# Second layer of a decoder trunk: the queries of three of eight heads formed by seven block products

## The chip, the cores and the metric

The kernel runs on one core of a Trainium2 chip. The metric is device time in microseconds (us) of one execution; a kernel is run several times and the median is given. Four engines matter here. TensorE (PE) multiplies matrices, and its weight loads have a row of their own in the profile (PEld). VectorE (DVE) and ScalarE (ACT) do elementwise work and alone empty the accumulators that TensorE writes. GpSimd (POOL) has a small part. SyncE (SP) issues most of the transfers (DMA).

## The reference

Sixteen learned meta tokens and 512 real ones, 1024 wide, pass through two layers with a residual, each behind an RMS norm: gated linear attention (GLA), then differential attention. A last RMS norm follows. The change lies in the second layer:

```python
proj = xn @ w_in                                  # 528 x 1024 by 1024 x 8192
q, k, v, z = jnp.split(proj, 4, axis=-1)          # 2048 columns each, 256 per head
s = einsum('bhpqd,bhpkd->bhpqk', qb, kh) * d**-0.5 + bias     # d = 128, p = 2 maps per head
p = softmax(s); a = p[:, :, 0] - lam * p[:, :, 1]
o = head_rms(a @ vh) * gnorm * (1 - lambda_init)
y = silu(z) * o;  h = h + y @ w_out
```

There are eight heads. A head has two query maps of 128 columns, and q of a head is the product of the normed tokens (1024 inputs) with 256 columns of `w_in`, scaled by -128 ** -0.5. Meta tokens need no queries in the second layer, as their output rows are dropped, so q has 512 tokens.

## The kernel before, in words

**Precision.** All products are of fp32 values split into a high part and a low rest, both in the type fp32r (`split`, L270). Three passes make a product: high by high, high by low, low by high.

**Two ways to form a projection.** The plain way is `project` (L414): the weights of 128 output columns lie in SBUF as a pair of tiles (high, low) of 8 slices, and for each slice three matmuls run over 512 token columns into one accumulator. A head's q has two such halves, 48 matmuls. The parts are prepared by `halves_of` (two pairs per load).

The other way is the class `Unit` (L436) over `product` (L428). The inputs are cut in two (512 of 1024), the output columns in two (128 of 256) and the tokens in two (an upper and a lower half). The 2 x 2 by 2 x 2 block product is then done by seven products of sums of blocks instead of eight products of blocks. Each product is 4 slices x 3 passes = 12 matmuls; its columns are half the tokens: 256 for real tokens only (the set `Xr`), 264 with the meta tokens (the set `X`). The sums of token blocks are made once for the layer. The sums of weight blocks are made for each unit by `want_unit` (L356): three single blocks (a11, a12, a22) are split, four additions on VectorE form sums, and two pairs of sums (s21, s43) are split. The products end in the accumulators bx, by and bv; `partial` copies three running results out of bx to tiles u on ScalarE (L452), and `add` combines accumulators and partials on VectorE into the output tile (L477, L479). When both token halves of one output block are there, `tail` is called. If the next piece of work in the queue is a unit too, its first product (a11) is issued ahead of the last two products of the running one.

**The order of the work.** TensorE's order is written out by the program. The projections stand in a queue as generators (the `Weaver`): each attention step of a head is emitted, and between two steps `W.fill` takes a number of microseconds of projection work, by the generators' own estimates, out of the queue. During head n the queue holds: the output projection of heads n-2 and n-1 (for n = 2, 4, 6), then z, v, k and q of head n+1; in head 6 the order is k, q, v, z. `W.stop` holds k and q back until the scores of head n are out, as k and q have one set of tiles. A head begins by finishing its own q (`W.finish(projs[hd])`), then takes 3.0 estimated us of the next work, and then emits its first scores, which need all of q and k. ScalarE, VectorE and the transfers are put in order by a planner from priorities: `at_once`, `urgent`, `soon` move an instruction 160, 100 or 40 places ahead of its place in the program.

**The weights.** `Weights` keeps the jobs in the order in which they are wanted. The two foremost are loaded into two buffers `raw`; their parts are made as soon as their buffers are free (two pairs, one sum, one each of a11, a12, a22), strictly in order. A transfer is issued from SP.

**The steps that are touched.** `q_diff_q` (L1650) forms q the plain way for all heads; each half is split straight out of its accumulator (ScalarE L279, VectorE L280). `q_diff_k` is a unit for heads 1 to 7 and shows what such a unit's ending looks like: `add` into temporary tiles `t` (three buffers, `tok_tile`), then `split` under `soon`. In this text heads are counted by index 0 to 7, so the fourth, sixth and eighth head are heads 3, 5 and 7, and their q are formed during heads 2, 4 and 6.

Of the kernel before, what the change touches and what calls it, by code (L numbers as in the profile page):

```python
# [12 lines left out]
F32R = mybir.dt.float32r  # L13
# [7 lines left out]
P = 128  # L21
# [3 lines left out]
NR = 512  # L25
# [184 lines left out]
def trunk(ctx, tc, x, meta, g_norm, gla_w_in, gla_w_gate_up, gla_b_gate, gla_gnorm, gla_w_out,  # L210
# [9 lines left out]
    d_w_in, d_lam, d_gn, d_w_out = diff_w_in[0], diff_lam[0], diff_gnorm[0], diff_w_out[0]  # L220
# [11 lines left out]
    def T(p, shape, dt, tag, **kw):  # L232
        uid[0] += 1
        return p.tile(shape, dt, tag=tag, name=f"{tag}_{uid[0]}", **kw)

    def pb_tile(tag):
        return T(pb_pool, [P, 512], F32, tag, bufs=2 if tag == "bx" else 1)
# [10 lines left out]
    def by_halves(t):  # L248
        return t.rearrange("p (n c) -> p n c", n=2)
# [4 lines left out]
    def urgent(fn, offset=100):  # L254

        def run(*a, **kw):
            with tc.high_priority(offset=offset):
                return fn(*a, **kw)
        return run
# [10 lines left out]
    def split(hi, lo, src, scale=None, keep=False):  # L270

        if keep:
            act.activation(hi, src, AF.Copy)
            kept.append(lambda: dve.tensor_tensor(lo, src, hi.bitcast(F32), op=ALU.subtract))
        elif scale is None:
            act.activation(hi, src, AF.Copy)  # L276
            dve.tensor_tensor(lo, src, hi.bitcast(F32), op=ALU.subtract)  # L277
        else:
            act.activation(hi, src, AF.Copy, scale=scale)  # L279
            dve.scalar_tensor_tensor(lo, src, scale, hi.bitcast(F32), op0=ALU.mult, op1=ALU.subtract)  # L280
# [21 lines left out]
    def block(raw, b):  # L302
        i, j = divmod(b, 2)
        return raw[:, 4 * j:4 * j + 4, i * P:(i + 1) * P]

    def in_rows(t):
        return t.rearrange("p (k c) -> p k c", c=P)

    W = Weaver()
# [22 lines left out]
    def halves_of(c):  # L332
        return [Part("pair", lambda raw, ca=ca: split_w(raw, ca)) for ca in (0, c)]
# [11 lines left out]
    def block_pair(src, keep=False):  # L345
        wh, wl = w_pair([P, 2, 512])
        if src.shape[1] == 2:
            split(wh, wl, src, keep=keep)
        elif src.shape[1] == 8:
            split(*[t.rearrange("p i (k c) -> p (i k) c", c=P) for t in (wh, wl)], src, keep=keep)  # L350
        else:
            split(*[t.rearrange("p i (k c) -> p i k c", c=P) for t in (wh, wl)],
                  src.rearrange("p k (i c) -> p i k c", c=P), keep=keep)
        return [[t[:, i, :] for t in (wh, wl)] for i in range(2)]

    def want_unit(w, c0, calm=False):  # L356
        def single(tag, b):
            def fn(raw):
                t = [T(wp, [P, 512], F32R, tag + part, bufs=1) for part in "hl"]
                with tc.issue_after(W.moved.ins) if calm and b == 0 else ExitStack():  # L360
                    split(*[in_rows(o) for o in t], block(raw, b))
                return t
            return Part(tag, fn)

        def add(o, a, b):
            dve.tensor_tensor(o, a, b, op=ALU.add)

        def sums(raw):
            t = T(wp, [P, 2, 512], F32, "sum", bufs=1)
            add(in_rows(t[:, 1, :]), block(raw, 2), block(raw, 3))  # L370
            add(in_rows(t[:, 0, :]), in_rows(t[:, 1, :]), block(raw, 0))
            add(block(raw, 2), block(raw, 2), block(raw, 0))
            return t

        def outer(raw):
            add(block(raw, 0), block(raw, 1), in_rows(su.t[:, 0, :]))
            ws.room["sum"] += 1
            return block_pair(raw[:, :4, :])

        a11, a12, a22 = single("a11", 0), single("a12", 1), single("a22", 3)  # L380
        su = Part("sum", sums)
        s21 = Part("pair", lambda raw: block_pair(su.t))
        s43 = Part("pair", outer)
        ws.want((w, c0), [a11, su, s21, a12, s43, a22])
        return a11, a12, a22, s21, s43
# [28 lines left out]
    def project(w, xs, n0, nn, banks, ks=range(KT)):  # L414

        (wh, wl), (xh, xl) = w.t, xs
        nk = wh.shape[1]
        todo = [(k, wh, b) for k in ks for b in (xh, xl)] + [(k, wl, xh) for k in ks]
        for n, (k, a, b) in enumerate(todo):
            for i, bank in enumerate(banks):  # L420
                pe.matmul(bank, a[:, k, :], b[k] if n0 is None else b[k][:, n0 + i * nn:n0 + (i + 1) * nn],  # L421
                          start=n == 0 and ks[0] == 0, stop=n == len(todo) - 1 and ks[-1] == nk - 1)
            if n % 3 == 2:
                yield 3 * len(banks) * max(nn / 2400.0, 0.107)
        if ks[-1] == nk - 1:
            ws.done(w)
# [211 lines left out]
    for b in range(5):  # L638
        t0, n = BLK[b]
        t = T(gp, [P, D], F32, ("qs", "ks")[b - 1]) if b in (1, 2) else {0: z2, 3: v2[0], 4: v2[1]}[b][:, 1, :]  # L640
# [134 lines left out]
    for k0 in range(0, KT, 2):  # L775
        if k0 + 2 < KT:
            scaled_pair(k0 + 2)
        i, ks = k0 // 4, slice(k0 % 4, k0 % 4 + 2)
# [204 lines left out]
    heads = [Head() for _ in range(G_HEADS)]  # L983
# [359 lines left out]
    for hd in range(G_HEADS):  # L1343
        s = heads[hd]
# [121 lines left out]
    def want_diff(c):  # L1466
        ws.want_in_order((d_w_in, 0, KT, c), halves_of(P))
# [29 lines left out]
    ep = ctx.enter_context(tc.tile_pool(name="ep", bufs=2))  # L1497
# [39 lines left out]
    Xr = {}  # L1537
# [8 lines left out]
    heads = [Head() for _ in range(D_HEADS)]  # L1546
# [16 lines left out]
    def tok_tile():  # L1563
        return T(ep, [P, 2 * (256 + NM)], F32, "t", bufs=3)
# [83 lines left out]
        return W.add(gen(), 10.3)  # L1648

    def q_diff_q(hd, s):  # L1650
        want_diff(256 * hd)

        def gen():
            for i in range(2):
                bank = pb_tile("bx" if hd else ("bv", "by")[i])
                yield from project(ws.take(), real2, None, NR, [by_halves(bank)])
                assert not hd or heads[hd - 1].scored
                if i == 0:
                    s.q = [T(ep, [P, 2, NR], F32R, f"q{j}", bufs=1) for j in range(2)]
                urgent(split)(*[t[:, i, :] for t in s.q], bank, scale=-float(P) ** -0.5)  # L1660
        return W.add(gen(), 10.3)

    def diff_steps(hd, s, ys):
# [156 lines left out]
    s = heads[0]  # L1820
# [5 lines left out]
    ws.room["sum"] += 1  # L1826
    s.T = bias_tile(0)
    q_diff_q(0, s)
    W.fill(2.5)
    for i in range(5):  # L1830
# [4 lines left out]
    for hd in range(D_HEADS):  # L1835
        last = hd == D_HEADS - 1
        s = heads[hd]
# [7 lines left out]
        if not last:  # L1845
            n = heads[hd + 1]
            late = hd == D_HEADS - 2
            if not late:
                gates.append(q_diff_z(hd + 1, n))
                values.append(q_diff_v(hd + 1, n))  # L1850
            W.stop = q_diff_k(hd + 1, n)
            projs.append(q_diff_q(hd + 1, n))
            if late:
                values.append(q_diff_v(hd + 1, n))
                gates.append(q_diff_z(hd + 1, n))
# [96 lines left out]
```

## Time and profile before

| | |
|---|---|
| median of 3 runs | 972.43 us (972.37 to 973.35) |
| profiled execution | span 970.2 us from first to last instruction; the page gives no other time of it |
| TensorE busy | 957.1 us (99%), 6993 matmuls |
| VectorE busy | 778.4 us (80%) |
| ScalarE busy | 628.0 us (65%) |
| matmuls of `project` with 512 columns, high weights, into bx (L421) | 224 |
| second layer, first scores of heads 0 to 7 | at 500.1, 552.3, 604.9, 678.7, 731.9, 805.3, 858.5, 913.1 us |

How to read it: busy time is the union of an engine's instructions. Matmuls overlap in the records (a row's length runs from its start to its modelled end), so the cost of one in a run is taken from start to start. A row `L431 PE MATMUL bx<-x,wh 128*128 128x256 f32 x8` reads: line 431, TensorE, into accumulator bx, from tiles x and wh, 128 by 128 weights, 256 columns, eight of them. In the list of waits a row names who waited, for whom, the total, the number and the longest, in us. In a table of stretches the numbers after the stretch are its length and each engine's busy time with its instructions, then the granted clock, the share of the transfer engines and GB/s.

### The profile page before, as it was taken

How to read it: one execution, taken by the hardware profiler on the slowest of the kernel's cores; microseconds unless marked ns; L12 is line 12 of the kernel's file. 1: busy time of each engine (PE TensorE's matmuls, PEld its weight loads, DVE VectorE, ACT ScalarE, POOL GpSimd, SP SyncE). 2: the span in 40 equal slices, each digit the busy share in tenths (PEclk: the TensorE clock that was granted, in tenths of full speed). 3: DMA queues.
4: the chain of work that ended last, by engine and by line, in shares of the span. 5: the costliest groups of instructions: out<-in, count | busy, mean ns of one | idle time of the engine just before them, and what ended most of it. 6: DMA issues, size and time to landing. Idle time of an engine off the chain costs nothing. (4 is left out here: it accounts for less than half of the span.)

```text
span 970.2 us, 18065 instructions
## 1 busy us (share of the span) xinstructions
PE 957.1 (99%) x6993; PEld 906.5 (93%) x6993; DVE 778.4 (80%) x1586; ACT 628.0 (65%) x1304; POOL 50.6 (5%) x68
## 2 busy tenths in 40 slices
PE   8999999999999999999999999999999999999997
PEld 8999999999999999898899998898998999989996
DVE  7989885886888887568997985977958879677785
ACT  7776755577647567656757774576764677655583
POOL 1000000000000100000001001001010000000001
PEclk9999999999999999999999999999999999999999
DMA  7322223635363245224355525135252352412212
GB/s 197 88 86 60 79 81 122 148 99 129 120 156 96 79 121 154 62 92 151 100 132 147 131 78 153 51 97 140 86 148 88 99 138 86 148 61 84 87 66 87
DMA packets 128521, 104.94 MB, mean 108 GB/s; under 512 B 51101, under 2 KB 112829, under 8 KB 128432
## 3 DMA queue, kind: packets, MB, share of 16 engines
q1 hardware_dynamic: 123104, 93.80, 35.1%
q10 hardware_dynamic: 5328, 9.95, 2.8%
q8 instruction: 56, 0.92, 0.4%
q14 instruction: 33, 0.27, 0.1%
HBM read 83.64 MB, written 11.80 MB: 98 GB/s over the span
## 5 line engine op out<-in xcount | busy, mean ns | idle before, releaser
L277 DVE TENSOR_TENSOR wl<-raw,wh 128x1024 fp32r<-128x1024 f32 x98 | 119.5, 1222 | 24.8 <-ACT wh L276 16.8
L276 ACT ACTIVATE wh<-raw 128x1024 fp32r<-128x1024 f32 x98 | 103.2, 1055 | 52.6 <-PE by L968 23.2
L431 PE MATMUL bv<-x,wh 128*128 128x264 f32 (+1 forms) x656 | 97.6, 286 | 0.0
L431 PE MATMUL bx<-x,wh 128*128 128x264 f32 (+1 forms) x640 | 94.9, 286 | 0.7 <-ACT u L452 0.6
L431 PEld LDWEIGHTS bv<-x,wh 128*128 128x128 f32 x656 | 86.5, 188 | 0.6 <-DVE z L479 0.3
L431 PEld LDWEIGHTS bx<-x,wh 128*128 128x128 f32 x640 | 84.5, 188 | 1.9 <-ACT u L452 1.2
L452 ACT ACTIVATE u<-bx 128x264 f32<-128x264 f32 (+1 forms) x120 | 45.4, 380 | 32.3 <-PE bx L431 31.1
L421 PE MATMUL bx<-x,wh 128*128 128x512 f32 (+1 forms) x256 | 62.4, 386 | 0.0
L277 DVE TENSOR_TENSOR wl<-sum,wh 128x1024 fp32r<-128x1024 f32 x41 | 50.1, 1221 | 14.3 <-ACT wh L276 13.9
L431 PE MATMUL bv<-x,wl 128*128 128x264 f32 (+1 forms) x328 | 55.2, 285 | 0.1
L1718 POOL TENSOR_TENSOR st<-st,mhalf 128x1 f32<-128x1 f32 x32 | 31.0, 970 | 464.4 <-ACT on L1716 408.9
L431 PE MATMUL bx<-x,wl 128*128 128x264 f32 (+1 forms) x320 | 53.9, 285 | 0.0
L1682 ACT ACTIVATE p<-p,st 128x528 f32<-128x528 f32 (+3 forms) x64 | 36.5, 571 | 25.4 <-DVE st L1680 24.9
L421 PEld LDWEIGHTS bx<-x,wh 128*128 128x128 f32 x256 | 44.5, 188 | 7.9
L276 ACT ACTIVATE wh<-sum 128x1024 fp32r<-128x1024 f32 x41 | 43.3, 1056 | 13.0 <-PE bv L431 4.0
L431 PE MATMUL by<-x,a12h 128*128 128x264 f32 (+1 forms) x320 | 46.5, 285 | 0.2 <-ACT t L1646 0.2
L431 PE MATMUL bx<-x,a11h 128*128 128x264 f32 (+1 forms) x320 | 46.3, 285 | 0.0
L431 PEld LDWEIGHTS bv<-x,wl 128*128 128x128 f32 x328 | 45.9, 188 | 0.4 <-issue 0.3
L431 PEld LDWEIGHTS bx<-x,wl 128*128 128x128 f32 x320 | 45.2, 188 | 0.6 <-DVE wl L277 0.2
L276 ACT ACTIVATE a11h<-raw 128x512 fp32r<-128x512 f32 x41 | 25.7, 627 | 28.6 <-DMA raw<-in_diff_w_in_dram 14.2
L431 PEld LDWEIGHTS bx<-x,a11h 128*128 128x128 f32 x320 | 42.2, 188 | 0.7
L431 PEld LDWEIGHTS by<-x,a12h 128*128 128x128 f32 x320 | 41.8, 188 | 0.4 <-ACT t L1646 0.4
(475 smaller groups left out, 2632.2 us busy)
## 6 DMA issues: line engine op xcount, KB each, us to landing
raw<-in_gla_w_in_dram SPq DMA_DIRECT2D x48, 512.0 KB, 4.5
raw<-in_diff_w_in_dram SPq DMA_DIRECT2D x42, 512.0 KB, 4.8
raw<-in_diff_w_in_dram SPq DMA_DIRECT2D x11, 1024.0 KB, 6.3
raw<-in_gla_w_out_dram SPq DMA_DIRECT2D x8, 1024.0 KB, 5.7
raw<-in_diff_w_out_dram SPq DMA_DIRECT2D x8, 1024.0 KB, 6.4
vd<-planes ACTq DMA_DIRECT2D x12, 268.0 KB, 7.1
vd<-keep ACTq DMA_DIRECT2D x12, 264.0 KB, 2.3
T<-bdr SPq DMA_DIRECT2D x8, 264.0 KB, 5.0
```

The costliest lines, as they stand in the source:

```text
L276: act.activation(hi, src, AF.Copy)
L277: dve.tensor_tensor(lo, src, hi.bitcast(F32), op=ALU.subtract)
L421: pe.matmul(bank, a[:, k, :], b[k] if n0 is None else b[k][:, n0 + i * nn:n0 + (i + 1) * nn], start=n == 0 and ks[0] == 0, stop=n == len(t ...
L431: pe.matmul(bank[:, :x[q].shape[2]], w[p][:, k * P:(k + 1) * P], x[q][:, k, :], start=first and i == 0, stop=i == len(PASSES) - 1, skip_gr ...
L452: W.moved = act.activation(t, self.bx[:, :self.n], AF.Copy, scale=self.sc)
L1682: act.activation(p[:, :nk], p[:, :nk], AF.Exp, scale=-1.0, bias=st[:, m:m + 1], accum_out=st[:, 2 + m:3 + m])
L1718: pool.tensor_tensor(ms, ms, mhalf[:, :1], op=ALU.pow)
```

## The change

For heads 3, 5 and 7, `q_diff_q` hands the queue a `Unit` over `Xr` in place of the plain generator. Its seven products of 256 columns go into two temporary tiles `t`, and its tail splits each of them into the q tiles under `soon`. The scale goes into the unit's partials and additions. The weights are asked for with `want_unit` in place of `want_diff`. Heads 0, 1, 2, 4 and 6 keep the plain way. The queue is told 8.9 us for the unit, where the plain generator is told 10.3.

```diff
     def q_diff_q(hd, s):
+        scale, qts = -float(P) ** -0.5, []
+
+        def tiles():
+            assert not hd or heads[hd - 1].scored
+            s.q = [T(ep, [P, 2, NR], F32R, f"q{j}", bufs=1) for j in range(2)]
+
+        if hd in (3, 5, 7):
+            def dst():
+                tiles()
+                qts.extend([tok_tile()[:, :NR], tok_tile()[:, :NR]])
+                return qts
+
+            @soon
+            def tail(i):
+                split(*[t[:, i, :] for t in s.q], qts[i])
+
+            return W.add(Unit(want_unit(d_w_in, 256 * hd), Xr, scale, dst, tail), 8.9)
         want_diff(256 * hd)
 
         def gen():
             for i in range(2):
                 bank = pb_tile("bx" if hd else ("bv", "by")[i])
                 yield from project(ws.take(), real2, None, NR, [by_halves(bank)])
-                assert not hd or heads[hd - 1].scored
                 if i == 0:
-                    s.q = [T(ep, [P, 2, NR], F32R, f"q{j}", bufs=1) for j in range(2)]
-                urgent(split)(*[t[:, i, :] for t in s.q], bank, scale=-float(P) ** -0.5)
+                    tiles()
+                urgent(split)(*[t[:, i, :] for t in s.q], bank, scale=scale)
         return W.add(gen(), 10.3)
```

## The prediction

> **What bounds the kernel now.** I read the page first: busy times, then the slices.
>
> ```profile
> span 970.2 us, 18065 instructions
> PE 957.1 (99%) x6993; PEld 906.5 (93%) x6993; DVE 778.4 (80%) x1586; ACT 628.0 (65%) x1304; POOL 50.6 (5%) x68
> PEclk9999999999999999999999999999999999999999
> ```
>
> TensorE works in 957.1 of 970.2 us at full granted clock. That share could still hide waits, so the second view is the list of who waited for whom, for TensorE alone; these are its rows that concern the second layer's projections.
>
> ```profile
> PE bx L421 <- DVE wl L277: 0.7, 1, 0.7
> ...
> PE bx L431 <- ACT u L452: 0.6, 2, 0.4
> ...
> PE by L431 <- ACT t L1646: 0.2, 1, 0.2
> ```
>
> Nothing to gain by feeding TensorE better: a projection gets cheaper only with fewer TensorE nanoseconds, and anything late at TensorE is a loss. So the third view is the busy time by stretch, cut at the first scores of head after head (by index 0 to 7; columns: stretch, its length, then PE, PEld, DVE, ACT, POOL busy). The new blocks would be formed in the stretches of heads 2, 4 and 6, as that is where the queries of heads 3, 5 and 7 (the fourth, sixth, eighth) are made.
>
> ```profile
> 500.10:552.30 52.20, 52.20 (x388) 49.72 (x387) 44.37 (x103) 36.98 (x88) 4.09 (x4) 1.00 0.66 153
> ...
> 604.90:678.70 73.80, 73.65 (x496) 67.94 (x495) 61.32 (x128) 47.95 (x103) 5.94 (x4) 1.00 0.35 101
> 678.70:731.90 53.20, 52.80 (x377) 49.54 (x376) 38.88 (x92) 34.22 (x82) 5.49 (x4) 1.00 0.40 114
> 731.90:805.30 73.40, 73.40 (x496) 67.95 (x495) 62.89 (x130) 48.55 (x104) 2.95 (x4) 1.00 0.38 103
> ...
> 858.50:913.10 54.60, 54.38 (x331) 48.25 (x330) 45.47 (x99) 32.29 (x78) 2.53 (x4) 1.00 0.26 82
> ```
>
> TensorE is full in each; VectorE is second with 83 to 86% in the affected three, and 85% (44.37 of 52.20) in the first, where TensorE lost nothing.
>
> **TensorE's term.** Before, a query pair is 2 halves x 8 slices x 3 passes = 48 matmuls of 512 columns. After, it is 7 products x 12 matmuls = 84 of 256 columns: 21,504 instead of 24,576 columns, an eighth less, but 36 more instructions and weight loads. Both shapes stand side by side in the order of time (start, length, engine, line):
>
> ```profile
> 542.99 3.88 PE L421 MATMUL bx<-x,wh 128*128 128x512 f32 x16
> 546.71 1.32 PE L421 MATMUL bx<-x,wl 128*128 128x512 f32 x5
> ...
> 548.79 1.11 PE L431 MATMUL bx<-x,a11h 128*128 128x256 f32 x8
> ...
> 550.20 1.11 PE L431 MATMUL by<-x,a12h 128*128 128x256 f32 x8
> ...
> 551.62 0.87 PE L431 MATMUL bx<-x,wh 128*128 128x256 f32 x6
> ```
>
> Lengths overlap, so I go from start to start. Sixteen matmuls of 512: 546.71 - 542.99 = 3.72, 232.5 ns each. Twelve of 256: 550.20 - 548.79 = 1.41 and 551.62 - 550.20 = 1.42, 117.9 ns each. Old 48 x 0.2325 = 11.16, new 84 x 0.1179 = 9.90: 1.26 less per head, **3.8 us** for three. Attention matmuls that cut into either are as many before as after. The bounds: query matmuls alone, in the three places, were busy
>
> ```profile
> 662.60:674.70 12.10, 11.79 (x48) 8.60 (x48) 1.00 0.59 142
> 789.60:801.70 12.10, 11.63 (x48) 8.79 (x48) 1.00 0.76 142
> 896.50:909.10 12.60, 12.04 (x48) 8.54 (x48) 1.00 0.26 83
> ```
>
> in sum 35.5 with their restarts after attention matmuls; against 3 x 9.90 that would be 5.8. From below, a unit can wait for its own partial result on ScalarE, as L431 did for u (above: twice, 0.4 at the longest): at 0.4 per head 2.6 remain. I take 3.8, as cuts fall on both forms alike and the list has two such waits in all of its units.
>
> One rule speaks against it. The Trainium skill, "TensorE: Matmul & The Clock Gate", section "Back-to-back issue gap", gives for streams of weight load and matmul a sustained 81 ns at 128 columns and 131 ns at 512; on a straight line between them (an estimate) 256 columns cost 98 ns, so 48 x 131 = 6.3 us would become 84 x 98 = 8.2, and the change would lose 5.8 us over three heads. The trace disagrees, with 232.5 and 117.9 ns; the measurement decides.
>
> **Work added beside it.** A block unit splits three single blocks (512 wide), forms four sums, and splits two pairs; the plain way splits two pairs of the same 1024 elements. It also writes three partial results on ScalarE and four additions on VectorE into a temporary tile, which is then split. The final split of 2 x 512 exists both ways. VectorE's steps, start to start:
>
> ```profile
> 607.91 0.69 DVE L366 TENSOR_TENSOR sum<-raw 128x512 f32<-128x512 f32 x1
> 608.52 0.68 DVE L277 TENSOR_TENSOR a12l<-raw,a12h 128x512 fp32r<-128x512 f32 x1
> ```
>
> give 0.61 for 512 wide, and the addition at 664.17 below is followed 0.34 later. VectorE gets 7 x 0.61 + 4 x 0.34 = 5.6 us per head. ScalarE's steps are these groups (count, busy time, mean in ns):
>
> ```profile
> L452 ACT ACTIVATE u<-bx 128x264 f32<-128x264 f32 (+1 forms) x120 | 45.4, 380 | 32.3 <-PE bx L431 31.1
> L276 ACT ACTIVATE a11h<-raw 128x512 fp32r<-128x512 f32 x41 | 25.7, 627 | 28.6 <-DMA raw<-in_diff_w_in_dram 14.2
> ```
>
> It gets three of each, 3 x 0.63 + 3 x 0.38 = 3.0, and is at 59 to 66%. VectorE goes from 61.3 of 73.8 to 66.9 of 72.5, 92%; 95% and 96% in the other two. Over a pair of heads it is (61.32 + 38.88 + 5.6) / (73.8 + 53.2 - 1.3) = 84%, no more than the stretch from 500.10 bore without a wait. So I cost it at nothing; it is hidden by VectorE's idle time, which in the part before the queries is large (the lower rows begin where k's last product ends):
>
> ```profile
> 631.00:662.60 31.60, 31.60 (x266) 31.56 (x265) 21.94 (x47) 22.88 (x51) 2.23 (x3) 1.00 0.40 124
> 662.60:678.70 16.10, 15.95 (x89) 13.47 (x88) 14.18 (x27) 10.39 (x22) 3.55 (x1) 1.00 0.45 107
> ...
> 789.60:805.30 15.70, 15.70 (x89) 13.49 (x88) 14.78 (x28) 10.66 (x22) 0.56 (x1) 1.00 0.60 112
> ...
> 896.50:913.10 16.60, 16.60 (x94) 14.14 (x93) 13.47 (x26) 9.64 (x22) 1.10 (x2) 1.00 0.26 84
> ```
>
> The first blocks of q can be prepared in the upper row's 9.7 idle us, since their buffers come free when k's own blocks are done. Without that cover the price is the second rival's.
>
> **Moves.** As q is now a unit, k's unit hands over to it: q's first product is issued ahead of k's last two, so its first block is needed two products, some 3 us, before 662.6. The weights were issued long before:
>
> ```profile
> 644.19 0.37 SPq L285 DMA_DIRECT2D raw<-in_diff_w_in_dram  x1
> 654.57 0.92 SPq L298 DMA_DIRECT2D raw<-in_diff_w_in_dram  x2
> ```
>
> 15 us of cover; the block form issues two transfers (0.92 on SP's queue for both) in place of one. Behind them on SP stand the transposes of v and the loads for the next head; those wait for k's last pair buffer either way. POOL has none of q's steps. Zero. The temporary tiles rotate through three buffers, and q's second takes the one that k's split frees, about 4 us after k's end (below); q's first addition comes three products after it, 3 x 1.41 = 4.2, so it just fits, and three more products follow before anybody needs its result. Zero again; late, it would hold up VectorE's queue behind it, the weight splits of the next z among them. In head 6, v is now the unit behind q, so v's first product moves ahead of q's last two as well: nothing added, 1.5 us of later filler spent earlier.
>
> **The tail of q** is the term that costs. The scores of the next head need q complete, and between q's last matmul and them lie about 30 filler matmuls:
>
> ```profile
> 674.69 1.11 PE L431 MATMUL bx<-x,a11h 128*128 128x256 f32 x8
> ...
> 677.84 0.98 PE L431 MATMUL bx<-x,wh 128*128 128x256 f32 x6 [0.15 <-ACT u L452]
> 678.66 1.61 PE L400 MATMUL ps<-k,q 128*128 128x264 f32 x12
> ```
>
> That is 3.97, of which 0.15 a wait: 3.82 of cover. By the ends of the stretches above it is 805.3 - 801.7 = 3.6 in head 4 and 913.1 - 909.1 = 4.0 in head 6. TensorE goes in program order, so whatever the scores wait delays everything behind them. Before, the last split ended at 677.44 + 0.69, 0.5 us ahead of the scores:
>
> ```profile
> 677.44 0.69 DVE L280 SCALAR_TENSOR_TENSOR q<-bx,q 128x512 fp32r<-128x512 f32 x1
> ```
>
> Now one more step (addition into the temporary tile) stands in front, and the split has a lower priority. The nearest rows are k's, the same code: k's last product ended at 662.6 in head 2, 842.1 in head 5 and 896.5 in head 6. These rows show what VectorE then did, in that order:
>
> ```profile
> 664.17 0.43 DVE L479 TENSOR_TENSOR t<-bv,u 128x264 f32<-128x264 f32 x1
> 664.51 0.68 DVE L277 TENSOR_TENSOR k<-t,k 128x512 fp32r<-128x512 f32 x1
> ...
> 666.47 0.17 DVE L277 TENSOR_TENSOR k<-t,k 128x16 fp32r<-128x16 f32 x1
> ...
> 842.12 1.08 PE L421 MATMUL bx<-x,wh 128*128 128x512 f32 x4
> ...
> 844.06 0.77 DVE L277 TENSOR_TENSOR k<-t,k 128x512 fp32r<-128x512 f32 x2
> ...
> 901.94 0.17 DVE L277 TENSOR_TENSOR k<-t,k 128x16 fp32r<-128x16 f32 x1
> ```
>
> The last splits ended at 666.64, 844.83 and 902.11: k was complete 4.05, 2.71 and 5.61 us after its product. With covers of 3.82, 3.6 and 4.0 that is nothing at 2.71; 0.23 + 0.45 + 0.05 = 0.7 at 4.05; 1.8 + 2.0 + 1.6 = 5.4 at 5.61. I take 4.05, the middle one and the one at the place of the change: **0.7**.
>
> **Sum.** -3.8 + 0.7 = -3.1 us. The profiled execution spans 970.2 and would span 967.1; the page gives no other time of it, and the median run of 972.43 is 2.2 above the span. What lies around stays: 972.43 - 3.1 = **969.3**.
>
> **Rivals.** *Late queries.* The tail is as slow as k's worst row in every place: -3.8 + 5.4 = +1.6, 974.0; break-even is a tail of 3.8 + 1.3 = 5.1 us. For it: VectorE is denser around q than around k. Against: q's split has no 16-column remainders, so two instructions fewer on each engine; two of three k rows lie below 5.1. About 972 where half of it comes.
>
> *VectorE becomes the bound* (the slower side). If none of the 5.6 us can be done ahead, the stretches from 662.60, 789.60 and 896.50 hold only 1.9, 0.9 and 3.1 idle us; the overflow is 3.7 + 4.7 + 2.5 = 10.9, the unit's blocks come late to TensorE, and the time is 972.43 + 10.9 = 983.3. It costs from the point where more than 2 + 1.3 us per head stay in that stretch. Against: the idle 9.7 us before it.
>
> *Weight loads bound the blocks*, the rule above as a mechanism: were a matmul's price the length of its weight load,
>
> ```profile
> L431 PEld LDWEIGHTS bv<-x,wh 128*128 128x128 f32 x656 | 86.5, 188 | 0.6 <-DVE z L479 0.3
> ```
>
> a head would cost 84 x 0.188 = 15.8, +13.9 for three, 986.3. The 256-column rows at 117.9 ns exclude it almost wholly.
>
> *The whole gain and more*: no late tail and the upper bound of TensorE's term: 972.43 - 5.8 = 966.6; with 3.8, 968.6.
>
> **Chances.** Forecast, 968.9 to 970.6: 0.57. The whole gain, below 968.9: 0.11. Late queries, 970.6 to 974.0: 0.20. VectorE bound: 0.11. Weight loads: 0.01. This kernel's measurement tells 0.2%, 1.9 us, from no change: faster means below 970.5, slower above 974.4. Faster 0.11 + 0.56 = 0.67; within: 0.01 of the forecast, the 0.20 of the late queries, 0.01 of a mild VectorE bound, 0.22; slower 0.10 + 0.01 = 0.11. The range 968.0 to 973.5 leaves out the upper end of the late queries and what lies above, some 0.13, and 0.04 below.
>
> **What would show it.** L421 at 512 columns falls by 144 matmuls, L431 at 256 gains 252, and start to start they keep 117.9 ns. The stretch of head 2 shrinks by about 1.0, those of heads 4 and 6 alike. A wait of TensorE's first scores (ps L400) for q's split on VectorE, of 0 to 0.5, is right; above 1.3 the late-query rival holds. Waits of L431 for VectorE's wl, a11l or sum would show the VectorE rival. I am wrong if the blocks run slower than 125 ns, or if new waits in heads 3, 5, 7 give the gain back.

## The result and the profile after

The changed kernel is slower: 979.25 us median of 5 runs (978.42 to 980.71) against 972.43 (972.12 to 973.35, 5 runs), a ratio of 1.0073 with a 95% interval of 1.0062 to 1.0084, 6.8 us. The forecast was 969.3 with a range to 973.5.

First the head of the page of the changed kernel: span, busy time by engine, granted clock in the last line.

```profile
span 977.5 us, 18336 instructions
PE 956.1 (98%) x7101; PEld 910.2 (93%) x7101; DVE 792.6 (81%) x1619; ACT 633.2 (65%) x1322; POOL 46.3 (5%) x68
PEclk9999999999999999999999999999999999999998
```

The span grew by 7.3 us, while TensorE's busy time fell by 1.0. The engine was given less to do and stood longer. Two of its groups by shape (count, busy time, mean in ns, idle time ahead and for whom):

```profile
L421 PE MATMUL bx<-x,wh 128*128 128x512 f32 x128 | 33.6, 400 | 0.0
L431 PE MATMUL bx<-x,wh 128*128 128x256 f32 x160 | 23.8, 284 | 1.7 <-ACT u L452 1.7
```

In the high-weight group of `project` 224 matmuls became 128; the blocks' group grew from 112 to 160. Their order of time (start, length, engine, line) in the new query products:

```profile
675.44 1.12 PE L431 MATMUL bx<-x,a22h 128*128 128x256 f32 x8
...
676.87 1.09 PE L431 MATMUL bv<-x,wh 128*128 128x256 f32 x8
...
678.27 1.10 PE L431 MATMUL bx<-x,a11h 128*128 128x256 f32 x8
```

Twelve matmuls of 256 columns take 1.43 and 1.40 us from start to start, 118 ns each, as forecast. The next view is busy time by stretch, cut at the first scores of head after head (columns as before: stretch, length, PE, PEld, DVE, ACT, POOL); the last row ends with TensorE's last matmul.

```profile
605.69:681.80 76.11, 72.66 (x531) 69.00 (x530) 65.21 (x137) 48.57 (x107) 4.05 (x4) 1.00 0.34 99
681.80:734.74 52.94, 52.92 (x376) 49.59 (x375) 40.12 (x94) 34.83 (x84) 2.98 (x4) 1.00 0.41 114
734.74:807.42 72.68, 72.64 (x532) 69.00 (x531) 64.55 (x135) 48.44 (x107) 3.48 (x4) 1.00 0.34 104
807.42:860.65 53.23, 53.06 (x376) 49.56 (x375) 40.42 (x95) 34.99 (x84) 2.82 (x4) 1.00 0.41 114
860.65:918.68 58.03, 55.12 (x379) 50.70 (x377) 49.75 (x108) 35.52 (x85) 2.24 (x4) 1.00 0.23 72
918.68:969.43 50.75, 49.33 (x329) 44.58 (x327) 38.22 (x94) 31.68 (x84) 4.13 (x7) 1.00 0.23 84
```

Before, cut at the starts of the first scores to 0.01 us, the stretches of heads 2 to 7 were 73.78, 53.23, 73.36, 53.27, 54.57 and 50.26. So head 4 behaves (-0.7), and the largest losses stand in two places: head 2, +2.3, where TensorE is idle for 76.11 - 72.66 = 3.45 us; and head 6, +3.5, idle for 2.9 (v's first product, 12 matmuls or 1.4 us, has moved into this stretch from head 7; that part is not a loss). Head 7, which gave that product away, grew by 0.5 all the same, so it lost some 1.9. Another 2.0 us of the span's 7.3 lie outside these stretches, 0.8 ahead of head 2 and 1.2 behind TensorE's last matmul; their cause stays open. Who waited for whom, TensorE alone:

```profile
PE bx L431 <- ACT u L452: 1.7, 1, 1.7
PE bv L431 <- DVE t L479: 1.7, 1, 1.7
...
PE ps L400 <- DVE v L576: 1.1, 1, 1.1
PE ps L1811 <- DVE x L277: 1.1, 1, 1.1
PE ps L400 <- DVE yt L1744: 0.9, 1, 0.9
...
PE ps L1727 <- DVE am L410: 0.5, 1, 0.5
```

The first two are head 2's, in the middle of the new query products, at 668.83 and 672.27; those for v, yt and am are head 6's attention, in code that the change does not touch; the one for x is in head 7. Two questions follow: why VectorE and ScalarE are late in head 2, and why an untouched head waits.

For the first, VectorE in the order of time in the changed kernel (in brackets: idle time ahead of the instruction, and for whom):

```profile
652.16 0.69 DVE L366 TENSOR_TENSOR sum<-raw 128x512 f32<-128x512 f32 x1 [2.31 <-DMA raw<-in_diff_w_in_dram]
...
664.84 0.69 DVE L366 TENSOR_TENSOR sum<-raw 128x512 f32<-128x512 f32 x1 [1.85 <-DMA raw<-in_diff_w_in_dram]
...
668.35 0.42 DVE L479 TENSOR_TENSOR t<-bv,u 128x264 f32<-128x264 f32 x1
668.69 0.68 DVE L366 TENSOR_TENSOR sum<-sum,raw 128x512 f32<-128x512 f32 x1
669.29 1.21 DVE L277 TENSOR_TENSOR wl<-raw,wh 128x1024 fp32r<-128x1024 f32 x1
```

The sum at 652.16 is the first preparation of q's weight blocks. Their transfer was issued here (the row joins four issues on SyncE; q's are the first two):

```profile
645.00 14.31 SPq L298 DMA_DIRECT2D raw<-in_diff_w_in_dram  x4
```

The sum sits early in VectorE's order, reaches the head of the queue before its transfer has landed, and VectorE, with work behind it that is ready, stands for 2.31 us. What stands behind in VectorE's queue is later by that, and at 664.84 VectorE stands again, 1.85 us, for the weights of the next unit (z). The addition that empties bv for k runs at 668.35, 4.2 us later than its counterpart before (664.17), and q's third product, which needs bv, waits until then. The second wait passes over two engines (GpSimd, then ScalarE twice):

```profile
668.64 2.28 POOL L1734 TENSOR_TENSOR st<-st,mhalf 128x1 f32<-128x1 f32 x1 [7.94 <-DVE k L277]
...
670.95 0.47 ACT L1735 ACTIVATE on<-ps,st 128x256 f32<-128x256 f32 x1 [1.85 <-POOL st L1734]
...
671.84 0.37 ACT L452 ACTIVATE u<-bx 128x256 f32<-128x256 f32 x1
```

GpSimd's power of 128 numbers takes 2.28 us, until just after VectorE's last row above ends (670.50); ScalarE stands behind it, and the partial result u, for which TensorE waits, is third in ScalarE's queue. A long power at this place is not new. The kernel before has this one:

```profile
667.04 3.55 POOL L1718 TENSOR_TENSOR st<-st,mhalf 128x1 f32<-128x1 f32 x1 [7.45 <-ACT on L1716]
```

ScalarE stood 4.07 us behind it there, and TensorE was idle for only 0.15 us in the whole stretch: plain q needs no partial result u from ScalarE. The unit does, and so the same delay now reaches TensorE.

### The profile page after: what moved, and what is told of

The parts are those of the page before. It is cut to its first block, busy times and chain, and to the rows that moved or that the text cites. A ratio compares the mean times of both kernels' runs of the same rounds, so it can differ in the third digit from the quotient of the medians.

```text
span 977.5 us, 18336 instructions
## 1 busy us (share of the span) xinstructions
PE 956.1 (98%) x7101; PEld 910.2 (93%) x7101; DVE 792.6 (81%) x1619; ACT 633.2 (65%) x1322; POOL 46.3 (5%) x68
## 5 line engine op out<-in xcount | busy, mean ns | idle before, releaser
L277 DVE TENSOR_TENSOR wl<-raw,wh 128x1024 fp32r<-128x1024 f32 x95 | 115.6, 1221 | 24.5 <-ACT wh L276 15.8
L431 PE MATMUL bv<-x,wh 128*128 128x264 f32 (+1 forms) x704 | 105.5, 287 | 1.8 <-DVE t L479 1.7
L431 PE MATMUL bx<-x,wh 128*128 128x264 f32 (+1 forms) x688 | 102.4, 286 | 1.9 <-ACT u L452 1.7
L431 PEld LDWEIGHTS bv<-x,wh 128*128 128x128 f32 x704 | 92.9, 189 | 2.8 <-DVE t L479 2.2
L431 PEld LDWEIGHTS bx<-x,wh 128*128 128x128 f32 x688 | 90.8, 188 | 3.1 <-ACT u L452 2.1
L277 DVE TENSOR_TENSOR wl<-sum,wh 128x1024 fp32r<-128x1024 f32 x44 | 53.7, 1221 | 16.8 <-ACT wh L276 16.7
L431 PE MATMUL bv<-x,wl 128*128 128x264 f32 (+1 forms) x352 | 58.2, 284 | 0.1
L431 PE MATMUL bx<-x,wl 128*128 128x264 f32 (+1 forms) x344 | 57.4, 285 | 0.0
L431 PE MATMUL by<-x,a12h 128*128 128x264 f32 (+1 forms) x344 | 50.1, 285 | 0.1
L431 PE MATMUL bx<-x,a11h 128*128 128x264 f32 (+1 forms) x344 | 50.1, 285 | 0.0
L431 PEld LDWEIGHTS bv<-x,wl 128*128 128x128 f32 x352 | 48.9, 188 | 0.3 <-issue 0.3
L1734 POOL TENSOR_TENSOR st<-st,mhalf 128x1 f32<-128x1 f32 x32 | 26.8, 836 | 474.2 <-ACT on L1732 435.5
L431 PEld LDWEIGHTS bx<-x,wl 128*128 128x128 f32 x344 | 48.2, 188 | 0.8 <-DVE wl L277 0.5
L431 PEld LDWEIGHTS bx<-x,a11h 128*128 128x128 f32 x344 | 45.2, 189 | 0.4
L431 PEld LDWEIGHTS by<-x,a12h 128*128 128x128 f32 x344 | 44.9, 188 | 0.4 <-ACT t L1646 0.3
L431 PE MATMUL by<-x,a22h 128*128 128x264 f32 (+1 forms) x264 | 38.4, 286 | 0.0
L366 DVE TENSOR_TENSOR sum<-raw 128x512 f32<-128x512 f32 x44 | 30.2, 687 | 9.9 <-DMA raw<-in_diff_w_in_dram 5.8
```

The costliest lines, as they stand in the source:

```text
L431: pe.matmul(bank[:, :x[q].shape[2]], w[p][:, k * P:(k + 1) * P], x[q][:, k, :], start=first and i == 0, stop=i == len(PASSES) - 1, skip_gr ...
L1734: pool.tensor_tensor(ms, ms, mhalf[:, :1], op=ALU.pow)
```

## The experiments

**One head at a time.** In each the condition `if hd in (3, 5, 7):` names one head.

> Block products for the fourth head (index 3) alone. Theory A (the loss is local: two waits of TensorE, 1.71 and 1.74 us, in the stretch of head 2, behind VectorE and ScalarE queues that stand on a weight transfer and on POOL): the stretch of head 2 is 2.0 to 2.6 us longer than before, with the same two waits at q's second and third products, and the rest of the second layer within 0.5 us of before: 974.3 to 975.5 in all. Rival B (the load of VectorE adds up over heads and the loss appears only with three heads): head 2 gains 1 us, 971.4.

> Block products for the sixth head (index 5) alone. Theory A (each place has its own sum): the stretch of head 4 is 0.5 to 1.0 us shorter than before, as in the kernel with all three, and nothing else moves: 971.4 to 972.0. Rival B (VectorE's load adds up): the same or better, 971.2, as nothing was piled up by head 2.

> Block products for the eighth head (index 7) alone. Theory A (local): the stretches of heads 6 and 7 together are 3 to 4.5 us longer than before, with the waits at the first values of head 6, at its last scores and at the last output product as in the kernel with all three: 975.5 to 977. Rival B (piled up from heads 2 to 5): they are 1.3 us shorter, 971.2.

Measured: fourth alone 974.95 us, ratio 1.0032 [1.0019, 1.0044]; sixth alone 974.78, 1.0028 [1.0017, 1.0038]; eighth alone 973.81, 1.0019 [1.0010, 1.0028]; before 972.07 beside them. 2.9 + 2.7 + 1.7 = 7.3, near the 6.8 of all three, but that agreement is luck, as the parts do not add by place: head 2 lost 0.4 with the fourth alone and 2.3 with all three, and head 5 lost 1.8 with the sixth alone and nothing with all three. Of the expectations, the first met its time by another route (head 6 in place of head 2), and the other two were missed (971.4 to 972.0 and 975.5 to 977). The stretches by head; fourth alone (head 2, head 6):

```profile
605.07:679.25 74.18, 72.65 (x531) 69.00 (x530) 64.69 (x136) 48.59 (x107) 2.32 (x4) 1.00 0.33 101
859.30:915.82 56.52, 55.01 (x331) 48.26 (x330) 45.15 (x99) 32.09 (x78) 2.20 (x4) 1.00 0.26 78
```

Head 2 of this run tells what the power is worth. In the last 25 us ahead of the next head's scores TensorE, VectorE and ScalarE run the same instructions in the same order as with all three heads. But the power, begun at 667.81, 0.06 us ahead of VectorE's next sum (0.05 with all three), took 0.55 us in place of 2.28. TensorE's wait for u did not come, the wait for bv did (1.5 us), and the stretch is 1.9 us shorter.

And sixth alone (heads 4, 5, 6):

```profile
732.34:804.48 72.14, 72.14 (x532) 68.90 (x531) 64.37 (x136) 49.05 (x107) 3.03 (x4) 1.00 0.37 104
804.48:859.55 55.07, 53.38 (x376) 49.66 (x375) 40.80 (x95) 34.80 (x84) 5.83 (x4) 1.00 0.40 111
859.55:916.17 56.62, 55.11 (x331) 48.31 (x330) 45.16 (x99) 32.02 (x78) 2.20 (x4) 1.00 0.25 78
```

Head 4's stretch shows the forecast gain undiminished: 73.36 to 72.14, -1.22. But head 6, in whose stretch nothing is changed in these two kernels, loses 1.95 and 2.05 us. Something is carried there from the heads before. It can be the engines' lateness, or the program's own account: a unit takes 28 steps of 0.33 = 9.24 us out of the queue (L428) and is told 8.9; the plain way takes 16 x 0.64 = 10.24 and is told 10.3. Each new unit leaves the account 0.34 short instead of 0.06 over; it is never settled, and from `W.left` the main loop works out how much projection work stands between two attention steps. (The z units of the kernel before are told 8.9 as well, so its account was short already; the change adds 0.40 for each unit of its own.)

**The eighth head with the old figure.**

```diff
-            return W.add(Unit(want_unit(d_w_in, 256 * hd), Xr, scale, dst, tail), 8.9)
+            return W.add(Unit(want_unit(d_w_in, 256 * hd), Xr, scale, dst, tail), 10.3)
```

> As the run with the eighth head alone, but the queue is told 10.3 us for the unit, as for the plain generator, so that the attention steps of heads 6 and 7 take as much filler between them as before. Theory C (the smaller estimate moves the attention steps of head 6 closer together, and what VectorE prepares for them comes late): the waits at the transposes, first values and last scores of head 6 fall below 0.3 us each, 972 to 974. Rival D (the unit's own weights and VectorE's load make these waits): they stay within 0.3 us of the run with 8.9, 975.5 to 977.

972.26 us, ratio 1.0003 [0.9994, 1.0012], against 973.81 with 8.9. TensorE in head 6 with 8.9:

```profile
873.53 0.38 PE L400 MATMUL ps<-v,aT 128*128 128x256 f32 x1
875.06 1.58 PE L400 MATMUL ps<-v,aT 128*128 128x256 f32 x11 [1.15 <-DVE v L576]
```

and with 10.3:

```profile
873.37 0.39 PE L400 MATMUL bx<-wh,hT 128*128 128x512 f32 x1
...
874.74 1.58 PE L400 MATMUL ps<-v,aT 128*128 128x256 f32 x12
```

The figure of 10.3 is 1.06 more than the unit spends, but until the unit has run the account stands as it did before the change. One more group of the output projection (six matmuls, 1.4 us) stands ahead of the value products, and the wait for v is gone. Head 6's stretch falls from 56.92 to 54.88 us. This loss in head 6 is not an engine's: the value products were dealt out one group too early for v's tokens to be there.

**The fourth head with a true figure, then with another order of products.** The first is told 9.3 (9.24 spent, the same 0.06 over as the plain way). The second also puts q's product on a12 (bank by) ahead of the one on the sums (bank bv):

```diff
+            if sc < 0:
+                before, after = (p2, p5), ()
```

> Only the fourth head's queries by seven products, and the queue is told 9.3 us for them instead of 8.9 (they spend 28 steps of 0.33 = 9.24). Theory of the estimate: with 8.9 the queue's count of work left ends 0.34 us too low per such unit and stays so, and the attention of the seventh head is dealt out closer; with 9.3 that goes, so the stretch of the seventh head (from its first scores to those of the eighth) falls from 56.5 us in the run with the fourth alone to 54.6 +- 0.3, its wait of 1.4 us before the value products is gone, and the time falls by about 1.9 us to 973.0. The stretch of the third head keeps its loss (74.2 against 73.8 before), because the wait for the bank bv is not touched. Rival, that VectorE and ScalarE carry a debt from the added work through the later heads: the estimate does not matter, the stretch of the seventh head stays at 56.5 and the time at 975.0.

> As the run before, and in the queries' products the one on the block a12 (bank by) goes ahead of the one on the sums of a21 and a22 (bank bv), so that two products instead of one lie between the keys' last product in bv and its next use. Theory of the bank: the wait of 1.66 us at about 668 us falls by one product (1.41 us) to at most 0.3, the stretch of the third head falls from 74.2 to 72.8 (the full -1.0 against before), and with the estimate's part the time is 971.5 +- 0.7, slightly under the kernel before. Rival, VectorE is behind with its work as a whole: the wait only moves to the next bank or to the queries' first scores, and the stretch of the third head stays at 74.0 or more (973.0).

The figure: 972.79 us, ratio 1.0002 [0.9993, 1.0011], expected 973.0. Its stretches of heads 2 and 6:

```profile
604.71:679.91 75.20, 73.06 (x531) 69.13 (x530) 64.24 (x136) 48.07 (x106) 3.96 (x4) 1.00 0.35 100
859.25:913.97 54.72, 54.49 (x331) 48.30 (x330) 45.35 (x99) 32.25 (x78) 2.53 (x4) 1.00 0.27 82
```

Its TensorE waits in head 2's stretch, the whole list:

```profile
PE bv L431 <- DVE t L477: 1.5, 1, 1.5
PE bv L431 <- DVE t L479: 0.5, 1, 0.5
```

And VectorE at the first of q's sums:

```profile
651.47 0.69 DVE L366 TENSOR_TENSOR sum<-raw 128x512 f32<-128x512 f32 x1 [3.81 <-DMA raw<-in_diff_w_in_dram]
```

Head 6 is back at 54.72. Head 2 was expected to keep its 74.2 and took 75.20, with the stall for the load at 3.81 us now (2.06 with 8.9) and TensorE's longer wait already in v's last product, ahead of any product of q; head 3 gave back 0.7. So the time met its number partly by luck. The other order made it worse, 974.79, ratio 1.0024 [1.0015, 1.0033], where 971.5 was expected, with head 2 at 76.18; its waits in that stretch:

```profile
PE bv L431 <- DVE t L477: 3.5, 2, 1.9
```

The theory of the bank fell: one wait is still that of v's last product (1.66), and one product of cover moved from one use of bv to the next, whose wait became 1.88 us. A lag of VectorE by more than a product cannot be covered by turning products round; its cause was still to be found.

**VectorE's sums held back.** With the figure 9.3, q's sums and first low part are put behind k's second pair in VectorE's order. TensorE's order stays the same, instruction for instruction. (`W.low` is the low part that `split` formed last; all three sums stand under `held`, and so does the split of a11.)

```diff
+        def held():
+            return tc.issue_after(W.paired.ins) if w is d_w_in and c0 in (768,) else ExitStack()
+
         def sums(raw):
             t = T(wp, [P, 2, 512], F32, "sum", bufs=1)
-            add(in_rows(t[:, 1, :]), block(raw, 2), block(raw, 3))
+            with held():
+                add(in_rows(t[:, 1, :]), block(raw, 2), block(raw, 3))
...
-            return block_pair(raw[:, :4, :])
+            pair = block_pair(raw[:, :4, :])
+            W.paired = W.low
+            return pair
```

> The fourth head's queries by seven products, told 9.3 us (as the run e5), and on VectorE the three sums and the first block's low part of the queries' weights are held until the low parts of the keys' second pair of blocks are formed; TensorE's order is the same instruction for instruction. Theory of the blocked queue: in e5 VectorE's first sum at 651.5 us stood 3.81 us for the weights' load, the keys' products' sums were behind it, and TensorE waited 1.50 us at 652.6 and 0.49 us at 668.4; with the sums held these waits go, the stretch of the third head falls from 75.2 to 73.3 +- 0.4 us and the time from 972.8 to 970.9 +- 0.6. Rival, VectorE has too much work in this stretch (73.2 us of busy time in 75.2): the order does not matter, the wait moves to a later product, the stretch stays at 74.7 or more and the time at 972.3 or more.

970.43 us, ratio 0.9978 [0.9969, 0.9987]; expected 970.9. The stretches of heads 2 and 6:

```profile
605.40:677.55 72.15, 72.15 (x531) 68.92 (x530) 64.34 (x136) 48.51 (x106) 3.86 (x4) 1.00 0.36 104
856.86:911.61 54.75, 54.52 (x330) 48.30 (x329) 45.34 (x99) 32.22 (x78) 2.53 (x4) 1.00 0.26 81
```

VectorE at q's first sum and at k's last addition (its lines have numbers six higher in this kernel):

```profile
655.93 0.69 DVE L366 TENSOR_TENSOR sum<-raw 128x512 f32<-128x512 f32 x1
...
665.54 0.42 DVE L485 TENSOR_TENSOR t<-bv,u 128x264 f32<-128x264 f32 x1
```

The first sum starts 4.5 us later than in e5 and waits for nothing; bv is emptied at 665.54 instead of 667.90, and TensorE waits for nobody in this stretch, 72.15 of 72.15, 1.63 less than before. VectorE's work in it is the same as in e5 (64.34 against 64.24 us), and on ScalarE the hold moved nothing: the high part of a11 starts at 650.07 in e9 and at 650.05 in e5. So the order of its queue was the cause, and the amount of its work was not.

**The sixth head's attention.** With the sixth alone, head 5 too had grown (55.07 against 53.27), and among the waits from 821 to 833 us were these:

```profile
ACT on L1735 <- POOL st L1734: 3.7, 1, 3.7
...
PE bv L431 <- DVE t L479: 1.4, 1, 1.4
```

GpSimd and VectorE at that place, in the order of time:

```profile
821.66 3.56 POOL L1734 TENSOR_TENSOR st<-st,mhalf 128x1 f32<-128x1 f32 x1 [29.35 <-ACT on L1732]
...
821.73 0.68 DVE L277 TENSOR_TENSOR a11l<-raw,a11h 128x512 fp32r<-128x512 f32 x1
...
824.14 0.68 DVE L366 TENSOR_TENSOR raw<-raw 128x512 f32<-128x512 f32 x1
```

The power took 3.56 us, under five VectorE instructions without a break, and ScalarE stood for it.

The first kernel below is told 9.3 and scales that head's output on VectorE, so that ScalarE does not stand behind the power; the second is told 9.3 only.

```diff
-            act.activation(r.on, po, AF.Copy, scale=ms)
+            if hd in (5,):
+                dve.tensor_scalar(r.on, po, ms, None, op0=ALU.mult)
+            else:
+                act.activation(r.on, po, AF.Copy, scale=ms)
```

> Only the sixth head's queries by seven products, told 9.3 us, and in the attention of the sixth head the scaling of the output by its norm (on <- ps, st) is done by VectorE instead of ScalarE. With the sixth alone (told 8.9, on ScalarE) the stretches of the fifth, sixth and seventh head were 72.1, 55.1 and 56.6 us against 73.4, 53.3 and 54.6 before. Theory of the power: GpSimd's power of 128 numbers took 3.56 us instead of 0.7 while VectorE ran without a break, ScalarE stood 3.73 us behind it and its next copies came late; without ScalarE in that chain the wait of 1.4 us of L431 for VectorE's t in the sixth head's attention goes and its stretch returns to 53.3 to 53.7. Theory of the estimate: the stretch of the seventh head returns to 54.6. Both: 971.0 +- 0.6. Rival, VectorE is simply the slower engine in the sixth head's attention: with 4 scalings more on it that stretch is 55.1 or longer; with the estimate's part alone 972.8 or more. VectorE itself now stands behind GpSimd's power, which may keep up to 1 us of the loss.

> As the run e7 (sixth head alone, told 9.3 us), with the scaling back on ScalarE. e7 had 972.65, 53.80 and 54.59 us for the stretches... of the fifth head 72.65, sixth 53.80, seventh 54.59, and 971.8 in all. Theory that ScalarE behind GpSimd's power was the cause in the sixth head's attention: its stretch goes back to 55.1 with a wait of about 1.4 us of L431 at about 832 us, and the time to 973.1. Rival, that it was the estimate (the deal of the fifth head's attention shifts when VectorE meets the power): the stretch stays at 53.8 or less and the time at 971.8 or less.

971.82 us (expected 971.0 +- 0.6), 0.9989 [0.9980, 0.9998], and 972.08, 0.9995 [0.9986, 1.0004]; head 5 took 53.79 and 54.01, head 6 54.60 and 54.59. Without the scaling the loss did not come back, so the second run's first theory fell; its rival's marks, 53.8 and 971.8 at most, were missed by 0.2 and 0.3. But the power itself was different there, with the scaling still on ScalarE:

```profile
822.18 0.57 POOL L1734 TENSOR_TENSOR st<-st,mhalf 128x1 f32<-128x1 f32 x1 [28.39 <-ACT on L1732]
```

It started 0.5 us later in much the same work of VectorE, and took 0.57 us where it had taken 3.56. Whether the long power alone made the 1.4 us of the sixth-alone kernel is not settled: for this place no run held everything else and took away only the power.

**Putting it together, and dividing the loss.** All three heads with the figures 9.3, 9.3, 10.3: with the order (e8), with the hold and the scaling (e11); sixth and eighth alone with the scaling (e12); then the change as made with the hold only (e13), with the figures only (e14), with both (e15); last the fourth and sixth with hold and scaling (e16).

> All three heads by seven products, told 9.3, 9.3 and 10.3 us, with the product on a12 ahead of the one on the sums in the queries. If the estimate and the bank are the larger parts of the loss: the stretches of heads three, five and seven fall to about 72.8, 72.1 and 54.9, the sixth's keeps its 53.2 to 55.1, the time is 971 +- 1.2 against 979.3 for the change as made and 972.1 before. If the added VectorE work is the loss: 976 or more. If only the estimate counts: about 975.

> All three heads, told 9.3, 9.3 and 10.3 us, the weights' sums of all three held on VectorE as in e9, and the sixth head's scaling on VectorE as in e7. If the losses are these three separate ones (estimate, blocked queue, ScalarE behind the power), they add: the third head's stretch 73.3, the fifth's 72.6, the sixth's 53.8, the seventh's 54.9, and the time is 972.1 - 0.5 - 0.7 + 0.4 = 970.5 +- 1.0, under the kernel before. If VectorE's load is the loss: the stretches of the third and fifth head stay at 74.5 or more and 73.4 or more, the time at 973.5 or more.

> The sixth and eighth head alone, told 9.3 and 10.3 us, the sixth head's scaling on VectorE; the fourth head's queries as before. The third head's stretch is that of before (73.8), the fifth's 72.65, the sixth's 53.8, the seventh's 54.9: by the sum of e7 (971.8) and of the eighth alone told 10.3 (972.3 against 972.1 before in that comparison) 971.8 to 972.1. If the seventh head's stretch, in which the eighth head's unit now runs behind another unit's changed drift, is dealt differently, up to 973.5.

> The change as made (told 8.9 for all three), with the sums and the first low part of the queries' weights held on VectorE in all three heads; TensorE's order is that of the change as made. Theory that the losses are two separate ones: the third head's stretch falls from 76.1 to 72.2 as in e9, the seventh's stays at 57.5 to 58.0, the time is 979.3 - 3.9 = 975.4 +- 0.8. Rival, one loss hangs on the other (VectorE late in one stretch carries into the next): the seventh's falls too, 973.5 or less; rival that the hold only helped in e9's deal of the steps: 977.5 or more.

> The change as made, told 9.3, 9.3 and 10.3 us, nothing held. Theory of two separate losses: the seventh head's stretch falls from 58.0 to 54.9, with the eighth's first scores, the third's stays between 75.2 (e5) and 76.1: 979.3 - 3.1 - 0.5 = 975.7 +- 1.0. Rival, the estimate is nearly all of it: 973 or less; rival, it counts for little beside VectorE's debt: 978 or more.

> Both mended and the sixth head's scaling on ScalarE as in the change as made. By the sum of the two: the third head's stretch 72.2, the fifth's 72.2, the sixth's 53.2 to 54.0, the seventh's 54.9 to 55.5, the time 970.4 +- 0.6, as e11, so that the scaling is worth nothing. If the scaling carried part of e11's time: 971.3 or more.

> The fourth and sixth head by seven products, told 9.3 us each, the queries' sums held on VectorE in both, the sixth head's scaling on VectorE; the eighth head as before. If the eighth takes back what the sixth gives: stretches 72.2, 52.6, 72.2, 53.8, 54.6 us for the third to the seventh head, time 970.4 - 0.7 = 969.7 +- 0.5, the fastest of all. If the sixth gives nothing in sum: 970.4 or more.

| kernel | us | ratio to before, 95% |
|---|---|---|
| change as made | 979.25 | 1.0073 [1.0062, 1.0084] |
| e8 figures, order | 975.18 | 1.0025 [1.0014, 1.0035] |
| e13 hold only | 976.47 | 1.0044 [1.0031, 1.0058] |
| e14 figures only | 973.79 | 1.0013 [1.0004, 1.0022] |
| e15 figures, hold | 971.36 | 0.9990 [0.9981, 0.9999] |
| e11 figures, hold, scaling | 970.37 | 0.9981 [0.9972, 0.9990] |
| e12 sixth, eighth; figures, scaling | 971.33 | 0.9989 [0.9980, 0.9998] |
| e9 fourth; figure, hold | 970.43 | 0.9978 [0.9969, 0.9987] |
| e16 fourth, sixth; figures, hold, scaling | 970.07 | 0.9973 [0.9962, 0.9983] |

e8 repeats e6's miss with all heads (975 instead of 971): with the figures mended, the order of products still costs 1.4 us against e14. e11 was expected at 970.5 and gave 970.37; e12 came out 0.5 us better than expected.

By ratios, against before, the figures alone take 6.0 points per mille off the 7.3 and the hold alone 2.9; both leave -1.0, which is 8.3 off and near their sum of 8.9. Taken off second, after the other, the figures are worth 5.4 points and the hold 2.3. The change as made thus lost more by the account (5.2 to 5.8 us) than by the blocked queue (2.2 to 2.8). e13 missed its number by 1.1 us: its head 2 fell to 72.39 as expected, but other waits came in head 5 (the first row) and head 4 (the second):

```profile
PE by L437 <- DVE a12l L277: 1.6, 1, 1.6
...
PE bx L437 <- ACT u L458: 1.1, 1, 1.1
```

In the first a part of a weight block is late; their causes were not followed further. e14 did better than expected by 1.9, with head 6 at 54.87 as forecast.

e15 expected 970.4 +- 0.6 and gave 971.36, which meets the mark set for the scaling carrying part of e11's time (971.3 or more). But in the traces (e15's is of an execution 0.9 us above its median), against e11, its fourth head's attention (head 3, which the scaling does not touch) took 54.00 us in place of 52.64, and there the power was long in e15:

```profile
695.78 2.56 POOL L1740 TENSOR_TENSOR st<-st,mhalf 128x1 f32<-128x1 f32 x1 [27.55 <-DVE sum L366]
```

In e11 the same instruction took 0.94 us, at 695.17. That speaks for a chance meeting and not for the scaling, but it is not shown, and the intervals of e11 and e15 overlap. Some of the differences of up to 1 us between these versions may be such chances. Six of them lie below the kernel before with their whole interval (e7, e12 and e15 barely); e9, e11 and e16 are the fastest, and their intervals don't tell them apart. e16's 970.07 lies within the expected 969.7 +- 0.5, so the eighth head adds nothing that can be seen to the other two; in e16's trace, of an execution 1.2 us above its median, head 2 took 72.92 where e9's took 72.15, and the question stays open within about 0.5 us.

## Why the prediction was wrong

- **TensorE's term, -3.8.** Right in price and in count: 118 ns per matmul of 256 columns, and, where nothing interfered, the stretch of head 4 in e2 fell by 1.22 us, against 1.26 per head. e9's -1.63 for head 2 lies between that and the upper bound. That the weight loads would not decide was right too.
- **Work added beside it, "I cost it at nothing".** This is the step that failed first. The amount was right (VectorE's busy time grew by 14.2 us over three heads, 4.7 each against 5.6) and the idle 9.7 us were there, but the step took idle time as cover without asking in what order the engine would use it. "The first blocks of q can be prepared in the upper row's idle us": they were placed there, ahead of their transfer, and VectorE stood for it with additions of v and k behind. The lateness, not the load, cost 3.45 us of TensorE in head 2, half of it by way of a long power that ScalarE stood behind, and moving the same instructions behind k's took it away: in e9 and e13 no wait of TensorE is left in head 2.
- **"Weights issued long before", zero.** The 15 us were counted from the issue to TensorE's first matmul. The unit's first preparation came to the head of VectorE's queue at 649.85 (652.16 less the 2.31 of idle time), 4.9 us after the issue at 645.00, and the data was there at 652.1. Cover ends at the first instruction that needs the data.
- **Moves.** The tile t rotated in time, as said. What was not in the list is bv: q's first use of it comes one product (1.4 us) after k's last, and k's addition was later than that. Also not in it is what the queue is told: 8.9 where 9.24 is spent. The text of the change had the figure, the prediction gave it no term, and it was the larger part of the loss (5.2 to 5.8 us), mostly in head 6, as e4, e5 and e14 show.
- **The tail of q, +0.7.** Not decisive: no wait of the scores for q is among those of the changed kernel; 0.2 us in the fourth-alone kernel and 0.4 in e4 lie inside its 0 to 0.5.
- **The rivals.** "VectorE becomes the bound" named the right engine and the right sign. Its mark was waits of L431 for wl, a11l or sum; those that came were for t and for ScalarE's u. Its mechanism, overflow of work, is refuted by e9, where the same work fits without a wait. Its threshold, "2 + 1.3 us per head", was also added the wrong way: when TensorE's stretch gets 1.3 us shorter, VectorE has less room in it, so the break-even with before lies at about 2 us per head. "Late queries" did not happen. That an account in the program could move an untouched head's work was no rival at all, and it should have been one: the change altered a number that all later heads are dealt by.

## What to carry to other kernels

An engine's idle time covers added work only if the added instructions come to its head when their data is there: ask for each one which transfer it needs, and what stands behind it in the same queue. Where a program deals out its work by estimates, an estimate that changes is an edit of everything dealt later; compare what is told with what is spent, and look for waits in stretches that the diff does not touch. Holding back an instruction that would reach the head of its queue ahead of its data can free the work that stands behind it, and an exchange of two products only moves a wait when the cause is an engine that is late.

## What the runs showed of the hardware

GpSimd's power of 128 numbers took 0.57 us in e10 and 2.28, 2.56 and 3.56 us in the three rows above where VectorE ran without a break; in the kernel before it took up to 3.55. In the long cases it ended with VectorE's streak: at 670.92 in the changed kernel, 0.42 us after 670.50, and at 825.22 in the sixth-alone kernel, 0.40 after 824.82. The Trainium skill, "SBUF — State Buffer", section "SBUF: two separate sides", says that a VectorE instruction with two inputs in SBUF and a GpSimd instruction that reads SBUF share a pair of ports, of which the one that starts first has the use to its end. The long rows agree with it, and add that GpSimd did not get in there between one such VectorE instruction and the next: it waited for the whole streak. That a busy VectorE always does this is not so, as the 0.57 us show, and e11's row: begun at 695.17 under a sum that ended at 695.70, the power ended at 696.11 while VectorE went on without a break. The fourth-alone kernel, with 0.55 us in the same order of instructions where all three heads had 2.28, suggests that hundredths of a us in the start decide; what decides is not shown. I had not expected that it reaches TensorE, by way of ScalarE's queue, as at 670.95 above, where it made the wait of 1.74 us that the fourth-alone kernel does not have.
